# Eight sevens in each down product's first block, seven low parts by transfer, and retention's rotations moved behind its own products

## The chip, the cores and the metric

The kernel runs on one core of a Trainium2 chip, in one launch. Times are device microseconds of that core; a profiled execution also has a span, from its first to its last instruction. Lower is better.

## What is computed

One decoder layer over 256 tokens of width 2048, all in float32:

```python
h = layer_norm(alpha*h + 0.5*swiglu(h, w_ffn1_gu, w_ffn1_down))      # d_ff 5632
rq, rk, rv, rg, aq, ak, av, gate_r, gate_a = split(h @ w_in)
rq, rk = rotary(rq), rotary(rk) * dk**-0.5                           # 8 heads of 128
ret = (silu(rg) * head_group_norm(retention(rq, rk, rv))) @ w_ret_out
att = windowed_attention(rotary(aq), rotary(ak), av, sinks) @ w_att_out
mixed = (sigmoid(gate_r)*ret + sigmoid(gate_a)*att) @ w_mix_out
h = layer_norm(alpha*h + mixed)
h = layer_norm(alpha*h + 0.5*swiglu(h, w_ffn2_gu, w_ffn2_down))
h = layer_norm(alpha*h + sigmoid(h @ w_ple_gate) * (p @ w_ple_proj))
# swiglu(x) = (silu(x @ w_g) * (x @ w_u)) @ w_down
```

## The kernel before

**Split products.** Each float32 operand is cut into a high part (rounded to the matmul's format) and a low part, the rest. A product is three matmuls summed in PSUM: high x low, high x high, low x high (`Sum.add`, lines 426 to 428; the names begin with `h` and `l`). Weights arrive as raw chunks of 128 x 1024 (512 KB, `Chunk`, line 115, on SP's queue). `split` (lines 101 and 102) has ScalarE cast the high part and VectorE subtract to get the low one.

**Units.** A product over pairs of k (256 rows of weights) is a list of units, and `block` runs them in order. Each pair covers two weight chunks (two column halves n), two k and two token halves:

- `P`, plain: two `Single`, 24 matmuls of 512 columns.
- `F`, folded: the second chunk is a `Folded`. Its low part comes not from VectorE but from a transfer: ScalarE casts the high part (line 165), writes its negative as the low part (line 166), and GpSimd issues a DMA that adds the raw chunk onto it inside SBUF (line 167).
- `S`, seven: the pair's 2 x 2 x 2 block products are made as seven products (21 matmuls) on sums of the weights (`Seven.make`: four additions on VectorE, lines 222 to 225, then 3.5 chunks' worth of high and low parts) and on combinations of the activations (`seven_forms`). Four of the seven go to PSUM banks of their own; after a block's last seven the `fold` (`seven_common`, lines 533 to 537, then line 1056) adds these onto the outputs. That last seven runs its steps in another order, so that those four end first.

**The order around a block.** `plan` lists all weight units of the whole kernel. `done(u)` after a unit frees its slots and calls `fill`, which loads and prepares units ahead: it prepares while less than 45 matmuls are ready, and loads while less than 90 are under way, both only if the slots of `slots_for_weights` allow it. SBUF has 46 slots of 4 KB per partition for weights, activations and everything temporary. Engines work in program order, so a preparation that waits for a slot holds up what stands behind it on ScalarE and VectorE.

**The down products** (`ffn`, tiles `f1d` and `f1e`, `f2d` and `f2e`). The 5632 rows are 22 pairs in 11 groups of activations. The output is made in two blocks of two column halves each. `down_units` gives the order of the pairs: the first block has twelve plain pairs, then five sevens and five plain pairs in turn, a plain one last; the second has two plain pairs, eight sevens and plain ones in turn, and the rest. Four groups (`SEVEN_DOWN`, pairs 12 to 19) have combinations, made by `before_unit` in front of units 2, 4, 6 and 8 of the first block. `before_unit` also cuts one group of activations into high and low parts (`convert`) in front of every second unit. After the first block VectorE adds the plain sums onto the residual (line 1078) and takes statistics (line 798).

**Beside the products** `run_side` runs, once per unit, the next job of `side` and a step of the first generator in `lazy`. In the first down product that is the table of retention's rotary angles (`rotary_table("r")`); in the mixers the sums of weights for the second feed-forward product, made ahead and put into DRAM (`sums_ahead`, 10 pairs, 8 of them here), and the table for attention. Retention's queries and keys (tile `rqk`) are rotated at the end of each of eight groups (`rotate`: joined from PSUM, shuffled, two products, one sum). Further on four pairs of gate sums (`sig`, line 1460) are copied out of PSUM on ScalarE.

## Time and profile before

| | |
|---|---|
| median of 3 runs | 2252.4 us (2251.03 to 2253.74) |
| the profiled execution: time, span | 2251.64 us, 2249.9 us |
| granted TensorE clock | 0.999 |
| busy: TensorE, VectorE, ScalarE, GpSimd | 99%, 88%, 63%, 2% |
| DMA: mean rate | 248 GB/s |
| low parts by transfer | 43, in the gate-and-up products |

In the lines below a number in front is a time or a window in microseconds from the span's start; `PE` is TensorE, `PEld` its weight load, `DVE` VectorE, `ACT` ScalarE, `POOL` GpSimd. `out<-in` names tiles with their buffer numbers left out, x is a count, and a bracket or an arrow at the end tells how long the engine had waited and for whom. In the list of waits the numbers are the total, the times, and the longest.

### The profile page before, as it was taken

How to read it: one execution, taken by the hardware profiler on the slowest of the kernel's cores; microseconds unless marked ns; L12 is line 12 of the kernel's file. 1: busy time of each engine (PE TensorE's matmuls, PEld its weight loads, DVE VectorE, ACT ScalarE, POOL GpSimd, SP SyncE). 2: the span in 40 equal slices, each digit the busy share in tenths (PEclk: the TensorE clock that was granted, in tenths of full speed). 3: DMA queues.
4: the chain of work that ended last, by engine and by line, in shares of the span. 5: the costliest groups of instructions: out<-in, count | busy, mean ns of one | idle time of the engine just before them, and what ended most of it. 6: DMA issues, size and time to landing. Idle time of an engine off the chain costs nothing.

```text
span 2249.9 us, 28922 instructions
## 1 busy us (share of the span) xinstructions
PE 2230.0 (99%) x10191; PEld 1845.7 (82%) x10191; DVE 1976.5 (88%) x2575; ACT 1406.5 (63%) x1640; POOL 39.7 (2%) x52
## 2 busy tenths in 40 slices
PE   9999999999999999999999999999999999999998
PEld 8888878888888888888778888888888778888887
DVE  6999999999989887888789778789999899889877
ACT  6777777766555444656776466456667677655533
POOL 0000000000000000000000000000000000000000
PEclk9999999999999999999999999999999999999999
DMA  9989998965677878767666578788989898555771
GB/s 321 244 270 254 246 257 239 256 220 186 220 284 260 292 282 306 223 239 231 187 189 234 178 229 296 301 283 274 315 271 294 275 250 262 188 215 210 286 266 72
DMA packets 292267, 557.14 MB, mean 248 GB/s; under 512 B 92045, under 2 KB 96525, under 8 KB 292121
## 3 DMA queue, kind: packets, MB, share of 16 engines
q1 hardware_dynamic: 283944, 530.16, 70.5%
q0 software_dynamic: 6192, 22.55, 5.3%
q10 hardware_dynamic: 1984, 2.58, 0.4%
q8 instruction: 80, 1.31, 0.2%
q14 instruction: 67, 0.54, 0.1%
HBM read 484.43 MB, written 29.36 MB: 228 GB/s over the span
## 4 chain that ended last, share of the span: by engine, by line
PE 75%; DVE 10%; DMA 6%; ACT 4%; issue 4%; SPq 0%; ACTq 0%; DVEq 0%; POOLq 0%
DMA lf_gu<-rf_gu 3%; PE rqk L377 3%; PE f1g L428 2%; PE f1g L427 2%; PE f1g L426 2%; PE f2g L427 2%; PE f2g L426 2%; PE f2g L428 2%; PE f1u L428 2%; PE f1u L427 2%; PE f2u L428 2%; PE f1u L426 2%; DVE lw_in_f L102 2%; PE f2u L427 2%; PE f2u L426 2%
## 5 line engine op out<-in xcount | busy, mean ns | idle before, releaser
L102 DVE TENSOR_TENSOR lf_gu<-rf_gu,hf_gu 128x1024 fp32r<-128x1024 f32 (+1 forms) x225 | 267.7, 1210 | 20.5 <-ACT hf_gu L101 19.7
L101 ACT CAST hf_gu<-rf_gu 128x1024 fp32r<-128x1024 f32 (+1 forms) x225 | 228.5, 1039 | 33.3 <-DMA rf_gu<-in_f_gu 32.9
L102 DVE TENSOR_TENSOR lf_down<-rf_down,hf_down 128x1024 fp32r<-128x1024 f32 x150 | 178.8, 1220 | 19.1 <-ACT hf_down L101 18.2
L102 DVE TENSOR_TENSOR lw_in_f<-rw_in_f,hw_in_f 128x1024 fp32r<-128x1024 f32 x140 | 167.4, 1219 | 28.2 <-ACT hw_in_f L101 27.7
L101 ACT CAST hf_down<-rf_down 128x1024 fp32r<-128x1024 f32 x150 | 151.9, 1049 | 49.3 <-DMA rf_down<-in_f_down 19.5
L101 ACT CAST huf_gu<-uf_gu 128x1024 fp32r<-128x1024 f32 x76 | 80.1, 1054 | 120.6 <-DVE uf_gu L223 111.9
L101 ACT CAST hw_in_f<-rw_in_f 128x1024 fp32r<-128x1024 f32 x140 | 140.2, 1049 | 5.2 <-PE rg L428 1.5
L101 ACT CAST hvf_gu<-vf_gu 128x1024 fp32r<-128x1024 f32 x76 | 80.1, 1054 | 32.1 <-DVE vf_gu L225 31.3
L102 DVE TENSOR_TENSOR luf_gu<-uf_gu,huf_gu 128x1024 fp32r<-128x1024 f32 x76 | 92.6, 1218 | 0.0
L102 DVE TENSOR_TENSOR lvf_gu<-vf_gu,hvf_gu 128x1024 fp32r<-128x1024 f32 x76 | 92.5, 1218 | 0.0
L426 PE MATMUL f1g<-hf_gu,xt 128*128 128x512 f32 x232 | 90.7, 391 | 0.0
L428 PE MATMUL f1g<-lf_gu,xt 128*128 128x512 f32 x232 | 90.5, 390 | 0.1
L427 PE MATMUL f1g<-hf_gu,xt 128*128 128x512 f32 x232 | 90.5, 390 | 0.0
L426 PE MATMUL f2g<-hf_gu,ht 128*128 128x512 f32 x214 | 83.5, 390 | 0.0
L428 PE MATMUL f2g<-lf_gu,ht 128*128 128x512 f32 x214 | 83.3, 389 | 0.0
L427 PE MATMUL f2g<-hf_gu,ht 128*128 128x512 f32 x214 | 83.3, 389 | 0.0
L428 PE MATMUL f1u<-lf_gu,xt 128*128 128x512 f32 x192 | 75.4, 393 | 4.1 <-DMA lf_gu<-rf_gu 4.1
L427 PE MATMUL f1u<-hf_gu,xt 128*128 128x512 f32 x192 | 74.7, 389 | 0.0
L426 PE MATMUL f1u<-hf_gu,xt 128*128 128x512 f32 x192 | 74.7, 389 | 0.0
L167 POOL DMA_DIRECT2D lf_gu<-rf_gu x43 | 37.3, 868 | 1852.8 <-DMA rf_gu<-in_f_gu 1240.9
L428 PE MATMUL f2u<-lf_gu,ht 128*128 128x512 f32 x168 | 66.0, 393 | 2.7 <-DMA lf_gu<-rf_gu 2.5
L426 PE MATMUL f2u<-hf_gu,ht 128*128 128x512 f32 x168 | 65.8, 392 | 0.0
(1471 smaller groups left out, 6788.9 us busy)
## 6 DMA issues: line engine op xcount, KB each, us to landing
rf_gu<-in_f_gu SPq DMA_DIRECT2D x360, 512.0 KB
rf_down<-in_f_down SPq DMA_DIRECT2D x176, 512.0 KB
rw_in_f<-in_w_in_f SPq DMA_DIRECT2D x148, 512.0 KB
lf_gu<-rf_gu POOLq DMA_DIRECT2D x43, 512.0 KB, 7.5
rw_rv<-in_w_rv SPq DMA_DIRECT2D x32, 512.0 KB
rw_ret<-in_w_ret SPq DMA_DIRECT2D x32, 512.0 KB
rw_mix<-in_w_mix SPq DMA_DIRECT2D x32, 512.0 KB
rw_pg<-in_w_pg SPq DMA_DIRECT2D x32, 512.0 KB
```

What stands on the lines that cost most here:

```text
L101: act.copy(dst_hi, src)
L102: (lo_engine or dve).tensor_tensor(dst_lo, src, dst_hi, ALU.subtract)
L167: pool.dma_start(c.lo, c.raw, accum_op=ALU.add)
L377: pe.matmul(ps[f], hi[:, kk, f * P : (f + 1) * P], rhs(k), start=k == 0, stop=k == n_k - 1,)
L426: pe.matmul(o, al, bh, start=first, stop=False)
L427: pe.matmul(o, ah, bh, start=False, stop=False)
L428: pe.matmul(o, ah, bl, start=False, stop=self.left == 0)
```

## The change

Both first blocks of the down products get the order `FIRST_DOWN`: six plain pairs, two folded, then eight sevens with a folded or plain pair between them; two of the sevens stand next to each other, and the block ends in a seven. Five of its pairs are folded. The second block keeps its eight sevens, moved back by one pair, and gets two folded pairs (`SECOND_DOWN`); its fold and tail stay. Groups of activations are converted four units (`LEAD`) before their first use, and the low part is issued behind the four combinations where both fall on one unit. `Folded.make` writes the negative from the raw chunk, issues the transfer, and casts the high part last; this holds for every folded unit of the kernel. The rotary table of retention is made in the mixers; the groups are only joined at their ends, and a second list of generators, `slow`, makes the table, then the rotations in place, then attention's table, one step per unit beside a step of `lazy`. The sums ahead are cut into three and five pairs. The last two of the four pairs of gate copies go to VectorE.

```diff
@@ -48,6 +48,10 @@
 
 SEVEN_DOWN = (6, 7, 8, 9)
 
+FIRST_DOWN = "PPPPPPFFSFSPSFSPSFSSPS"
+SECOND_DOWN = "PPPSPSPSFSPSFSPSPSPPPP"
+LEAD = 4
+
 BIG = 3.0e38
 MAGIC = 12582912.0
 INV_2PI = 0.15915494309189535
@@ -162,9 +166,9 @@
         def make(self):
             c = self.chunk
             c.make_hi()
+            act.mul(c.lo, c.raw, -1.0)
+            pool.dma_start(c.lo, c.raw, accum_op=ALU.add)
             act.copy(c.hi, c.raw)
-            act.mul(c.lo, c.hi.bitcast(F32), -1.0)
-            pool.dma_start(c.lo, c.raw, accum_op=ALU.add)
 
     class Turn:
 
@@ -356,15 +360,16 @@
         room["quiet"] = on
 
     side = []
-    lazy = []
+    lazy, slow = [], []
     idle = lambda: None
 
     def run_side(n=1):
         for _ in range(n):
             if side:
                 side.pop(0)()
-        if lazy and next(lazy[0], "end") == "end":
-            lazy.pop(0)
+        for jobs in (slow, lazy):
+            if jobs and next(jobs[0], "end") == "end":
+                jobs.pop(0)
 
     def features_chunk(key, n_k, rhs, ps):
         c, chunks = key[-1], n_k // 4
@@ -489,7 +494,7 @@
             if p == sevens[-1]:
                 fold(p1.ap, p6.ap, p7.ap, q5.ap)
 
-    def seven_forms(full, hi, lo):
+    def seven_forms(full, hi, lo, between=None):
 
 
         a11, a21 = (full[:, 0::2, t * P : (t + 1) * P] for t in range(2))
@@ -500,6 +505,8 @@
         dve.tensor_tensor(f7, a11, a21, ALU.subtract)
         dve.tensor_tensor(f6, f5, a11, ALU.subtract)
         dve.tensor_tensor(f3, a12, f6, ALU.add)
+        if between is not None:
+            between()
         split(hi, lo, raw)
         return lambda e: [(hi[:, 2 * j + e, :], lo[:, 2 * j + e, :]) for j in range(4)]
 
@@ -918,24 +925,16 @@
     def down_units(n_held):
 
 
-        first = [("P", p) for p in range(2 * SEVEN_DOWN[0])]
-        g = SEVEN_DOWN[0]
-        sevens = [2 * h for h in SEVEN_DOWN[:3]] + [2 * SEVEN_DOWN[2] + 1, 2 * SEVEN_DOWN[3]]
-        plain = [p for p in range(2 * g, KF // 2) if p not in sevens]
-        plain = [p for p in plain if p < 2 * SEVEN_DOWN[2]] + sorted(
-            (p for p in plain if p >= 2 * SEVEN_DOWN[2]), key=lambda p: p < 2 * SEVEN_DOWN[3] + 2
-        )
-        while sevens or plain:
-            for kind, of in (("S", sevens), ("P", plain)):
-                if of:
-                    first.append((kind, of.pop(0)))
-        plain = [p for p in range(KF // 2) if p // 2 not in SEVEN_DOWN]
-        second = [("P", p) for p in plain[:2]]
-        rest = plain[2:]
-        for g in SEVEN_DOWN:
-            for e in range(2):
-                second += [("S", 2 * g + e), ("P", rest.pop(0))]
-        return first, second + [("P", p) for p in rest[:-n_held]], rest[-n_held:]
+        sevens = [2 * g + e for g in SEVEN_DOWN for e in range(2)]
+        plain = [p for p in range(KF // 2) if p not in sevens]
+        first, second = [], []
+        for out, order in ((first, FIRST_DOWN), (second, SECOND_DOWN)):
+            n = order.count("S")
+            of = {"S": sevens[:n], "P": sorted(plain + sevens[n:], key=lambda p: (p in sevens, p))}
+            of["F"] = of["P"]
+            out += [(kind, of[kind].pop(0)) for kind in order]
+            assert not of["S"] and not of["P"]
+        return first, second[:-n_held], [p for _, p in second[-n_held:]]
 
     def down_keys(name, b):
         return lambda n, p: (name + "_down", 2 * b + n, p)
@@ -973,10 +972,14 @@
 
         acts = {}
 
+        def convert_high(g):
+            hi, lo = (slot([P, 4, S], F32R, f"{name}a{w}{g}") for w in "hl")
+            act.copy(hi, raws[g])
+            acts[g] = hi, lo
+            return lambda: dve.tensor_tensor(lo, raws[g], hi, ALU.subtract)
+
         def convert(g):
-            hi, lo = (slot([P, 4, S], F32R, f"{name}a{w}{g}") for w in "hl")
-            split(hi, lo, raws[g])
-            acts[g] = hi, lo
+            convert_high(g)()
 
         for j in range(KF // 4):
             pg, pu = banks(f"{name}g{j}"), banks(f"{name}u{j}")
@@ -1056,17 +1059,27 @@
                     dve.scalar_tensor_tensor(x, x, 2.0 * ALPHA, v, ALU.mult, ALU.add)
             return f
 
+        when = {}
+        for at, (kind, p) in enumerate(first):
+            if p // 2 > 1:
+                when.setdefault(p // 2, max(0, at - LEAD))
+
         def before_unit(u):
-            if u == 0 and name == "f1":
-                lazy.append(rotary_table("r"))
-            g = u // 2 + 2
-            others(2 * KF // 4 - max(0, KF // 4 - 1 - g) + (2 if u >= 10 else 0))
-            if u % 2 == 0:
-                if 2 <= u < 2 + 2 * len(SEVEN_DOWN):
-                    at = u // 2 - 1
-                    made[SEVEN_DOWN[at]] = seven_forms(raws[SEVEN_DOWN[at]], space[:, 2 * at], space[:, 2 * at + 1])
-                if g < KF // 4:
-                    convert(g)
+            new = [g for g in when if when[g] == u]
+            others(2 * KF // 4 - (KF // 4 - len(acts) - len(new)) + (2 if u >= 10 else 0))
+            lows = [convert_high(g) for g in new]
+
+            def convert_low():
+                for f in lows:
+                    f()
+
+            if u % 2 == 0 and 2 <= u < 2 + 2 * len(SEVEN_DOWN):
+                at = u // 2 - 1
+                made[SEVEN_DOWN[at]] = seven_forms(
+                    raws[SEVEN_DOWN[at]], space[:, 2 * at], space[:, 2 * at + 1], convert_low
+                )
+            else:
+                convert_low()
             if u in (11, 12):
                 y[u - 11] = load_columns(residual, u - 11, name + "y")
 
@@ -1121,14 +1134,16 @@
             dve.tensor_tensor(v[:, f], ps[f][:, :S], lo[:, f], ALU.add)
         return v
 
-    def rotate(ps, name, dst, cos, sin, shuffle):
-        q = joined(ps, name)
+    def turn_by_angle(q, name, dst, cos, sin, shuffle):
         qs = half(name + "sh")
         dve.stream_shuffle(qs, q, shuffle)
         c, s = (v[:, None, :].broadcast_to([P, 2, S]) for v in (cos, sin))
         dve.tensor_tensor(q, q, c, ALU.mult)
         dve.tensor_tensor(qs, qs, s, ALU.mult)
         dve.tensor_tensor(dst, q, qs, ALU.add)
+
+    def rotate(ps, name, dst, cos, sin, shuffle):
+        turn_by_angle(joined(ps, name), name, dst, cos, sin, shuffle)
 
     SH_R = [(i + 16) % 32 for i in range(32)]
     SH_A = [i + 8 if i < 8 else i - 8 if i < 16 else i for i in range(32)]
@@ -1170,7 +1185,6 @@
         side.insert(n, job)
 
     def mixers(ht, norm, residual, keepers, away):
-        cos_r, sin_r = trig["r"]
         rhs = lambda k: (ht[:, k, :S], ht[:, k, S:])
         both_halves = lambda k: ht[:, k, :]
         rq = [slot([P, 4, S], F32, f"rq{j}") for j in range(2)]
@@ -1178,7 +1192,20 @@
 
         def rotated(grp, ps):
             who = (rq, rk)[grp // 4][grp % 4 // 2]
-            rotate(ps, f"rr{grp}", who[:, grp % 2 * 2 : grp % 2 * 2 + 2, :], cos_r, sin_r, SH_R)
+            to = who[:, grp % 2 * 2 : grp % 2 * 2 + 2, :]
+            joined(ps, f"rr{grp}", to)
+            unturned[grp] = to
+
+        unturned = {}
+
+        def rotations():
+            for grp in (0, 4, 1, 5, 2, 6, 3, 7):
+                while grp not in unturned:
+                    yield
+                to = unturned.pop(grp)
+                turn_by_angle(to, f"rr{grp}", to, *trig["r"], SH_R)
+                yield
+                yield
 
         rv = []
 
@@ -1201,10 +1228,14 @@
         values(0, ps)
         slots_for_weights(14)
         ahead = [(gu_keys("f2", j)(0, p), gu_keys("f2", j)(1, p)) for j in AHEAD for p in AHEAD[j]]
-        lazy.append(sums_ahead(ahead[:2], 3, 2))
-        lazy.append(rotary_table("a"))
-        lazy.append(sums_ahead(ahead[2:5], 2, 2))
-        lazy.append(sums_ahead(ahead[5:8], 2, 3))
+        def angles():
+            yield from rotary_table("r")
+            yield from rotations()
+            yield from rotary_table("a")
+
+        slow.append(angles())
+        lazy.append(sums_ahead(ahead[:3], 3, 2))
+        lazy.append(sums_ahead(ahead[3:8], 2, 2))
         for grp in range(8):
             ps = banks(f"rqk{grp}")
             features_out([(("w_in_f", grp), ps)], KD, both_halves)
@@ -1457,7 +1488,7 @@
             paired_out(("w_in_f2", 21 + 2 * j), KD, rhs, ps, before)
             sig.append(slot([P, 2, 512], F32, f"sig{j}"))
             for t in range(2):
-                act.copy(sig[-1][:, t], ps[t])
+                (act.copy if j < 2 else dve.tensor_copy)(sig[-1][:, t], ps[t])
         assert not side
 
         def mixer_block(name, units, keys, lhs):
```

## The prediction

> **What bounds the kernel now.** First the page: span, then busy time.
>
> ```profile
> span 2249.9 us, 28922 instructions
> PE 2230.0 (99%) x10191; PEld 1845.7 (82%) x10191; DVE 1976.5 (88%) x2575; ACT 1406.5 (63%) x1640; POOL 39.7 (2%) x52
> ```
>
> TensorE is busy 2230.0 of 2249.9 us. Time can therefore go in two ways only: fewer matmuls, or fewer of its few waits. The waits of TensorE, longest first:
>
> ```profile
> PE f1u L428 <- DMA lf_gu<-rf_gu: 4.1, 6, 1.8
> PE ao L1423 <- ACT apt L197: 3.2, 2, 2.5
> PE f2u L428 <- DMA lf_gu<-rf_gu: 2.5, 3, 1.8
> ```
>
> Two of the three largest are waits for the low part that comes by transfer (`lf_gu<-rf_gu`, the folded unit): 4.1 us in 6 and 2.5 us in 3, none over 1.8 us. The third, the attention's 3.2 us, the change leaves alone.
>
> Then the stages around the edits (columns: window, length, then busy us and count of PE, PEld, DVE, ACT, POOL, the granted clock, DMA share, GB/s). 240 to 463.6 is part of the first gate-and-up product; 463.6 to 694 and 1915.8 to 2147 are the two down products, first and second block; 720 to 814 retention's query and key products, 1156 to 1237 the gate blocks.
>
> ```profile
> 240.00:463.60 223.60, 220.42 (x969) 181.19 (x968) 207.49 (x245) 166.20 (x177) 12.97 (x15) 1.00 0.89 252
> 463.60:579.90 116.30, 116.30 (x515) 96.30 (x514) 107.97 (x135) 72.22 (x76) 0.00 (x0) 1.00 0.60 203
> 579.90:694.00 114.10, 114.10 (x505) 94.49 (x504) 105.53 (x125) 61.53 (x66) 0.00 (x0) 1.00 0.71 253
> 720.00:814.00 94.00, 94.00 (x533) 82.37 (x533) 83.77 (x121) 45.71 (x60) 0.00 (x0) 1.00 0.82 295
> 1156.00:1237.00 81.00, 81.00 (x359) 67.05 (x358) 79.78 (x95) 52.46 (x59) 0.00 (x0) 1.00 0.65 215
> 1915.80:2032.00 116.20, 116.20 (x514) 96.24 (x513) 102.36 (x116) 71.17 (x74) 0.00 (x0) 1.00 0.57 200
> 2032.00:2147.00 115.00, 115.00 (x513) 95.23 (x512) 106.80 (x128) 61.49 (x68) 0.00 (x0) 1.00 0.69 248
> ```
>
> TensorE is at 100% in all but the first, at clock 1.00. VectorE follows closely: 107.97 of 116.30, 105.53 of 114.10, 83.77 of 94.00, 79.78 of 81.00. So matmuls are what is to be saved, and VectorE is what can spoil it.
>
> **Part 1: three more sevens in each first block.** A plain pair is 24 matmuls of 512 columns (two weight chunks, two k, two token halves, three products for the split), a seven is 21.
>
> ```profile
> L426 PE MATMUL f1d<-hf_down,f1al x141: 389/389/389, 463.8 to 579.4; 128*128 128x512 f32 x141
> L426 PE MATMUL f1e<-hf_down,f1al x120: 389/389/389, 580.1 to 693.7; 128*128 128x512 f32 x120
> ```
>
> A matmul's 389 ns is its pipelined length. Its spacing is what counts: the first block, 17 x 24 + 5 x 21 = 513 matmuls by the code, begins at 463.8 and the next at 580.1, so 116.3 / 513 = 0.227 us each. The first block goes from five sevens to eight in both products; the second keeps eight and only changes order. 2 x 3 x 3 x 0.227 = **4.1 us less**.
>
> What VectorE pays (timeline of VectorE, start and length):
>
> ```profile
> 560.69 0.69 DVE L222 TENSOR_TENSOR uf_down<-rf_down,rf_down 128x512 f32<-128x512 f32 x1
> ...
> 567.36 2.35 DVE L102 TENSOR_TENSOR lf_down<-rf_down,hf_down 128x1024 fp32r<-128x1024 f32 x2
> ...
> 1957.33 0.42 DVE L499 TENSOR_TENSOR sums<-f2a 128x256 f32<-128x256 f32 x1
> ```
>
> A seven's preparation runs from 560.69 to 567.36, 6.7 us, the pair behind it 2.35 us (about 2.3 without the overlap): 9.0 us of VectorE for 45 matmuls, 10.2 us of TensorE. A transferred low part takes 1.1 us off a pair. For one product: 3 x (6.7 - 2.3) - 7 x 1.1 = +5.5 us. In the first product the rotary table leaves: 107.97 against 102.36 for the same work in the second says 5.6 us. VectorE then has about 213 of 228 us in the first product and 215 of 229 in the second: it fits on average. The dense place is the last 14 units of the first block: eight sevens (53.4), three plain (6.8), three folded (3.4), five low parts of activations (5.7) and one set of combinations (four of 0.42 and a subtraction, 2.8) make 72.1 us against (8 x 21 + 6 x 24) x 0.227 = 70.7 us. It falls behind by 1.4 us there, from whatever lead it has. How much that is:
>
> ```profile
> 569.90 0.39 PE L426 MATMUL f1d0s<-hf_down,f1al 128*128 128x512 f32 x1
> 569.91 2.00 ACT L101 CAST hf_down<-rf_down 128x1024 fp32r<-128x1024 f32 x2 [1.48 <-PE f1d L427]
> ```
>
> The seven prepared by about 567.4 starts at 569.90: 2.5 us of lead, and its last sums are read only after 17 matmuls, 3.9 us later. ScalarE at 569.91 had waited for TensorE, that is for slots: the preparation had run as far ahead as it could. 2.5 + 3.9 covers 1.4. I charge nothing for it; without that lead it costs what the third rival says.
>
> **Part 2: the block now ends in a seven.** Until now a plain pair stood behind the last seven and hid its fold; now the fold meets the next block's start.
>
> ```profile
> 573.27 0.59 ACT L533 COPY eve<-f1d0s 128x512 f32<-128x512 f32 x1 [1.35 <-PE f1d L427]
> 573.89 0.69 DVE L534 TENSOR_TENSOR evw<-eve,f1d0s 128x512 f32<-128x512 f32 x1 [0.53 <-ACT eve L533]
> 578.81 2.35 DVE L102 TENSOR_TENSOR lf_down<-rf_down,hf_down 128x1024 fp32r<-128x1024 f32 x2
> 581.08 2.48 DVE L1078 TENSOR_TENSOR f1y<-f1y,f1d 128x512 f32<-128x512 f32 x4
> 583.47 2.46 DVE L798 BATCH_NORM_STATS2 f1st<-f1y 128x6 f32<-128x512 f32 x4
> 585.85 0.67 DVE L222 TENSOR_TENSOR uf_down<-rf_down,rf_down 128x512 f32<-128x512 f32 x1
> 574.43 0.39 PE L428 MATMUL f1d<-lvf_down,f1ah 128*128 128x512 f32 x1
> 580.10 0.39 PE L426 MATMUL f1e<-hf_down,f1al 128*128 128x512 f32 x1
> ```
>
> The seven's last matmul issues at 574.43, so the unit ends at 574.66; the fold's copy had started 1.4 us before that, its six VectorE operations take 573.89 to 578.81, 4.9 us. The next block starts at 580.10, before the additions of the plain sums (581.08): its banks are those that the fold has freed, not those. With nothing between, its first matmuls need the bank of the copy (free at 573.86, in time) and 0.7 us later one more; the fold's second sum ends 573.89 + 1.4 = 575.3, 0.6 us after the unit: even. If instead that bank waits for all four sums (until 576.5), each product loses 1.2 us. I take 0.3 each, 0 to 1.2 the range. Behind it queue 2.5 us of additions, 2.5 us of statistics and two plain low parts: 4.2 + 4.9 + 2.3 + 6.7 = 18.1 us after the block's end for the next seven, which starts after three plain pairs, 16.3 us, and is read to its end 3.9 us later. 2.1 us are left.
>
> **Part 3: the folded unit's order.** The sign change now comes before the high copy, and the transfer starts one ScalarE operation earlier, in all 43 old folded units.
>
> ```profile
> 309.73 1.04 ACT L165 CAST hf_gu<-rf_gu 128x1024 fp32r<-128x1024 f32 x1
> 310.80 1.06 ACT L166 ACTIVATE lf_gu<-hf_gu 128x1024 fp32r<-128x1024 f32 x1
> 312.22 0.86 POOL L167 DMA_DIRECT2D lf_gu<-rf_gu  x1 [17.55 <-ACT lf_gu L166]
> 321.79 0.50 PE L428 MATMUL f1u<-lf_gu,xt 128*128 128x512 f32 x1 [1.81 <-DMA lf_gu<-rf_gu]
> 322.12 0.39 PE L426 MATMUL f1u<-hf_gu,xt 128*128 128x512 f32 x1
> DMA to landing us min/median/max: 4.9/7.5/10.3
> L167 POOL DMA_DIRECT2D lf_gu<-rf_gu x43: 859/862/1010, 41.6 to 1890.6; - x43
> ```
>
> Copy at 309.73, sign change at 310.80, issue at 312.22, read at 321.79 after 1.81 us of wait. Each transfer starts 1.07 us sooner (310.80 - 309.73). Of nine waits that add up to 6.6 us, none over 1.8, two keep about 0.75 us each and the others end: 5.1 us. A wait also hides 0.16 us that the profile counts as busy (389 - 227 ns) and is followed by one matmul 0.1 us late (322.12 - 321.79 - 0.23); seven such ends give 1.8 us more. Together 6.9 us if every landing moves with its start; 0 if none does. I take **6 us less**. The high part comes 1.06 us later than now, but still some 9 us ahead of the low one: nothing waits for it.
>
> The Trainium skill (DMA: Bandwidth & Descriptors, "Anatomy of one DMA — SWDGE (gpsimd) path") fits such a transfer at 2.0 us plus bytes over 436 GB/s, as an estimate 3.2 us for 512 KB. The trace disagrees: 4.9 to 10.3 us. By that page no folded unit would wait at all, and the new ones in the down products would cost nothing.
>
> Those are 14 new transfers. From the start of the sign change to the landing is 1.06 + 0.36 + 4.9 to 10.3 us; the next ScalarE cast waits for none of it. Second chunks are cast about 9 to 11 us before use (569.91 for 580.10), so most arrive in time, in a stage whose DMA share is 0.57 to 0.71. Bounds: 0, and 14 x 1.8 = 25 us if each waited as long as the worst old one; near the old rate after the shift (2 of 43) and some more for the shorter lead I take 0.8 us. POOL issues nothing else there; its issue took 859 to 1010 ns under a busy VectorE, so there is no queue to be behind.
>
> **Part 4: the rotations and the gate copies.** The first product's table leaves work that had no wait, so no time there.
>
> ```profile
> 737.65 0.74 DVE L1127 STREAM_SHUFFLE rr0sh<-rr0v 128x512 f32<-128x512 f32 x1
> 740.37 2.35 DVE L102 TENSOR_TENSOR lw_in_f<-rw_in_f,hw_in_f 128x1024 fp32r<-128x1024 f32 x2
> 1185.49 1.22 DVE L102 TENSOR_TENSOR lvw_in_f<-vw_in_f,hvw_in_f 128x1024 fp32r<-128x1024 f32 x1
> 1187.89 0.39 PE L428 MATMUL ga0s<-lvw_in_f,gaf1h 128*128 128x512 f32 x1
> ```
>
> A rotation is 740.37 - 737.65 = 2.7 us of VectorE. Into the stage of 720 to 814 come the retention table (5.6 us) and about one and a half more of the sums made ahead (four operations of 0.69 and two of 1.22 each, 7.8 us), which no longer pause for the attention's table; that table (5.6) and two rotations (5.4) fall behind the stage. 83.8 + 2.4 = 86.2 of 94 us, though its last groups carry two rotations each. TensorE had no wait there (94.00 of 94.00); 0 to 2 us now, I take 0.3. DMAs move with it: a small load of positions on ScalarE's queue, and on SP's the loads and stores of those sums, between weight loads, in a stage with a DMA share of 0.82. Two of the four pairs of gate copies go to VectorE; the last pair (2 x 0.69 us, the length of the fold's L534 on as many elements) lands ahead of the fullest stage, 79.78 of 81.00, whose last seven is ready at 1186.7 and read at 1187.89: 1.2 us of room for 1.4 us. Between no cost (ScalarE is freed of as much, and VectorE's next operation waits for its cast) and 1.4 us, I take 0.3, nearer to the row with the room.
>
> **The sum.** -4.1 - 6 + 0.6 + 0.8 + 0.3 + 0.3 = -8.1 us. The profiled execution took 2251.64 us, 1.74 more than its span and 0.76 less than the median of the runs, 2252.4; so 2243.5 on its own scale, **2244.3 us** as a median.
>
> **Rivals.** *The landing stays.* If transfers are held by what else the 16 engines carry (share 0.89 in the gate-and-up product) and not by their start, part 3 gives about 0.5 us and the rest stands: 2252.4 - 4.1 - 0.5 + 2.0 = 2249.8 us. For it: landings spread by 5.4 us. Against it: waits of at most 1.8 us behind transfers that differ this much look like the tail of one spread, and a shift of all cuts a tail. The Trainium skill says of the same page ("Issuing engines are not separate DMA queues") that transfers of every queue interleave on the same 16 engines; the spread agrees with that.
>
> *Added waits eat the gain.* The 14 transfers late by 0.3 us each, both boundaries at 1.2 and the mixers at 2: 4.2 + 2.4 + 2.3 against 10.1 leaves 2251.2 us.
>
> *VectorE is late in the dense stretch.* Low parts that come by transfer hold their raw slot until they land, up to 10.3 us; if the sevens' preparation waits for those slots, the lead of 2.5 us is gone when the stretch begins. Then its 1.4 us and the 9.8 us of fold, additions and statistics stand before the next seven uncovered, less 3.9 us: 7.3 us per product, 14.6 in all, 2244.3 + 14.6 = 2258.9 us. It decides once VectorE idles more than the lead, about 2.5 + 3.9 us, within the stretch. For it: ScalarE's wait for slots at 569.91. Against it: with 9.0 of 10.2 us per couple, VectorE caught up after each seven.
>
> **How the numbers follow.** Forecast 0.68, landing stays 0.12, waits eat the gain 0.10, VectorE late 0.10. The forecast's own cases run from 2241 (6.9 us, no new waits: -11 us) to 2248; the range goes up to 2251.5 to take in the next two. A measurement of this kernel tells about 0.2%, 4.5 us, from no change: faster than 2247.9 is the forecast and a little of the next, 0.70; slower than 2256.9 is the last, 0.09; the same 0.21.
>
> **What would show it.** In the changed profile: 9 matmuls fewer in each first block, which should last about 114.3 us; TensorE's wait for `lf_gu` near 1.5 us instead of 6.6, and no `lf_down` in that list above 1 us; at the end of each first block a gap under 1.2 us; no wait of TensorE in retention's products. Wrong would be: waits for `luf_down` or `lvf_down` (third rival), waits for `lf_gu` as before with the transfers 1.07 us longer (first), or a gap of several us before the second block.

## The result and the profile after

The changed kernel takes 2247.37 us in the median (2246.52 to 2252.30), the kernel before, run beside it, 2254.99 us (2251.03 to 2258.21): 7.6 us less between the two medians. The ratio of the runs is 0.9971 with a 95% interval of 0.9962 to 0.9980, which is 6.5 us less (4.5 to 8.6); the experiments below are compared by this ratio. The forecast was 8.1 us less (2252.4 to 2244.3).

The changed kernel's page and its waits of TensorE (in total, times, longest, us):

```profile
span 2248.5 us, 29078 instructions
PE 2230.2 (99%) x10173; PEld 1846.2 (82%) x10173; DVE 1987.0 (88%) x2601; ACT 1421.7 (63%) x1662; POOL 51.7 (2%) x66
PE f27s L433 <- DVE lf_gu L106: 2.1, 1, 2.1
PE lnps L684 <- DVE f2y L672: 1.0, 2, 0.6
PE lnps L684 <- DVE f1y L672: 0.9, 2, 0.5
PE gt L433 <- DVE lw_in_f L106: 0.8, 1, 0.8
PE f1u L433 <- DMA lf_gu<-rf_gu: 0.8, 1, 0.8
PE f27s L433 <- DVE luf_gu L106: 0.8, 1, 0.8
PE f2u L433 <- DMA lf_gu<-rf_gu: 0.4, 1, 0.4
```

TensorE executes fewer matmuls and waits little for `lf_gu`: 0.8 and 0.4 us, where 4.1 and 2.5 stood. But there are new names: `f27s` (pair 7's sevens in the second gate-and-up product) waits 2.9 us for VectorE, the layer norms' `lnps` 1.9 us for `f1y` and `f2y`, and `gt` 0.8 us for VectorE. The stages that were shown of before:

```profile
240.00:459.30 219.30, 219.30 (x969) 181.61 (x968) 206.47 (x245) 164.18 (x177) 12.93 (x15) 1.00 0.91 257
459.30:573.60 114.30, 114.30 (x506) 94.65 (x505) 105.53 (x123) 80.63 (x85) 4.33 (x5) 1.00 0.71 222
573.60:688.70 115.10, 114.67 (x505) 94.30 (x503) 105.36 (x126) 62.62 (x68) 1.72 (x2) 1.00 0.75 264
1913.90:2028.20 114.30, 114.30 (x506) 94.66 (x505) 105.31 (x123) 80.61 (x85) 4.33 (x5) 1.00 0.71 223
2028.20:2141.60 113.40, 112.66 (x496) 92.67 (x494) 105.12 (x125) 62.32 (x67) 1.91 (x3) 1.00 0.74 256
```

Both first down blocks last 114.3 us instead of 116.3 and 116.2; TensorE is full in them. The second blocks now have a gap at the end (114.67 of 115.10, 112.66 of 113.40), which the kernel before had not (114.10 of 114.10, 115.00 of 115.00).

The profiled execution took 2250.32 us, 3 us over its median, and that of before 2251.64 us, 3.4 us under its own. So the two spans differ by 1.4 us only, and the stages tell more. Lengths in us, from a stage's first matmul to the next one's (e1 has the folded unit's new order alone, e12 is the fastest version found; both come below):

| stage | before | after | e1 | e12 |
|---|---|---|---|---|
| first gate-and-up product | 458.48 | 454.00 | 454.21 | 454.18 |
| its down product, first block | 116.28 | 114.24 | 116.30 | 114.24 |
| second block and norm | 145.23 | 146.95 | 145.23 | 145.95 |
| retention | 326.12 | 325.36 | 326.10 | 325.35 |
| gates and gate blocks | 185.63 | 187.94 | 187.06 | 186.57 |
| rest of the mixers | 222.45 | 222.36 | 222.48 | 223.06 |
| second gate-and-up product | 456.45 | 457.79 | 456.70 | 456.63 |
| its down product, first block | 116.28 | 114.24 | 116.28 | 114.24 |
| second block, up to the gate's product | 115.16 | 117.39 | 115.17 | 115.17 |
| to the end | 102.44 | 102.93 | 102.45 | 102.42 |

In the changed kernel's column 1.6 us in the gates and 3.2 us in the second gate-and-up product are a halved clock that only some executions have at these places (last section); the gates of e1 and e12 hold 1.6 us of it too. Without it the changed kernel has: 4.5 less in the first product, 4.1 less in the first blocks, 0.8 less in retention, 1.9 less in the second product, 3.95 more in the second blocks with their norms, 0.7 more in the gates, 0.4 more after them. About 6 us less.

### The profile page after: what moved, and what is told of

It is laid out like the page before. It is cut to its first block, busy times and chain, and to the rows that moved or that the text cites. A ratio compares the mean times of both kernels' runs of the same rounds, so it can differ in the third digit from the quotient of the medians.

```text
span 2248.5 us, 29078 instructions
## 1 busy us (share of the span) xinstructions
PE 2230.2 (99%) x10173; PEld 1846.2 (82%) x10173; DVE 1987.0 (88%) x2601; ACT 1421.7 (63%) x1662; POOL 51.7 (2%) x66
## 4 chain that ended last, share of the span: by engine, by line
PE 90%; DVE 4%; DMA 3%; issue 2%; ACT 1%; ACTq 0%; POOL 0%; DVEq 0%; POOLq 0%
PE rqk L382 3%; PE f1g L431 3%; PE f1g L432 3%; PE f1g L433 3%; PE f2g L431 2%; PE f2g L432 2%; PE f2g L433 2%; PE f1u L433 2%; PE f1u L431 2%; PE f1u L432 2%; PE f2u L433 2%; PE f2u L431 2%; PE f2u L432 2%; PE aqk L382 2%; PE f1d L433 1%
## 5 line engine op out<-in xcount | busy, mean ns | idle before, releaser
L106 DVE TENSOR_TENSOR lf_down<-rf_down,hf_down 128x1024 fp32r<-128x1024 f32 x130 | 155.5, 1220 | 14.5 <-ACT hf_down L105 13.9
L105 ACT CAST hf_down<-rf_down 128x1024 fp32r<-128x1024 f32 x130 | 132.8, 1049 | 38.3 <-DMA rf_down<-in_f_down 26.9
L105 ACT CAST huf_down<-uf_down 128x1024 fp32r<-128x1024 f32 x32 | 33.7, 1053 | 57.2 <-DVE uf_down L227 55.2
```

What stands on the lines that cost most here:

```text
L105: act.copy(dst_hi, src)
L106: (lo_engine or dve).tensor_tensor(dst_lo, src, dst_hi, ALU.subtract)
```

## Experiments

The theory after this comparison: the folded unit's order carries the gain, and the down orders give back at the norms what they save. The rivals were that the landings would stay, that the parts work only together, and that VectorE's whole load, not the place of single steps, makes the new waits. Ratios below are to the kernel before, with 95% intervals.

**e1: the folded unit's order alone.**

```
-            act.copy(c.hi, c.raw)
-            act.mul(c.lo, c.hi.bitcast(F32), -1.0)
+            act.mul(c.lo, c.raw, -1.0)
             pool.dma_start(c.lo, c.raw, accum_op=ALU.add)
+            act.copy(c.hi, c.raw)
```

> Only the folded unit's new order (sign change, transfer, then high copy), on the kernel before. Theory (waits shrink with the earlier start): TensorE's waits for lf_gu fall from 6.6 us in nine to 1 to 2 us, and the time falls by 4 to 6 us, less what VectorE's own lateness in the second gate-and-up product takes back (0 to 2 us, seen as a longer wait of f27s for lf_gu from VectorE). Rival, the landing stays: the transfers last 1.07 us longer, the waits for lf_gu stay above 5 us, and the time falls by 0.5 us.

Measured: 2246.84 us, ratio 0.9969 (0.9959 to 0.9980): 7.0 us less, as much as the whole change brings and a little more than the 4 to 6 us expected. Its waits for `lf_gu` fall to 3.5 us, not to the 1 to 2 us expected:

```profile
PE f2u L428 <- DMA lf_gu<-rf_gu: 2.7, 3, 1.2
PE f1u L428 <- DMA lf_gu<-rf_gu: 0.8, 2, 0.4
```

The time from issue to landing of the `lf_gu` transfers hardly grew (e1's row follows: count, size, median us; before and in the changed kernel it is 7.5). The median is 0.3 us longer, not the 1.07 us of the earlier start, so the landings moved with their start, and the rival falls.

```profile
lf_gu<-rf_gu POOLq DMA_DIRECT2D x43, 512.0 KB, 7.7
```

The gain is not spread as the waits were. Over the profiled executions of this study with 46 shared slots the first gate-and-up product lasts 459.3 us with the old order (four, 458.2 to 460.7, one of them with 1.6 us of halved clock) and 454.0 with the new one (eight, 453.8 to 454.2); the second lasts 456.5 with either. There the folded waits stay in e1 (2.7 us), and in the changed kernel 2.9 us at `f27s` stand in their place. e9 asks why. So the traces place 5 of the 7 us; where the other 2 come from stays open.

**e2: the down orders alone** (`FIRST_DOWN`, `SECOND_DOWN`, `LEAD`, the low parts by transfer; old folded order; rotary table, rotations and gate copies as before).

> Only the down products' orders (eight sevens, seven plain pairs by transfer, the conversions' new lead), with the folded unit's old order, and the rotations and gate copies as before. Prediction's terms: each first block 2.04 us shorter, about 114.3 us, boundary 0.3 each, new transfers 0.8 in all: 2.7 us less altogether. Theory after the changed kernel's trace: both first blocks at about 114.3 us, but each second block with the layer norm behind it 1 to 1.7 us longer (waits of lnps for f1y and f2y), so only 1 to 2 us less altogether. Rival (the 14 transfers, starting 1.07 us later here than in the changed kernel, are late): waits of TensorE for lf_down in the first blocks of 0.3 us or more each, and no gain at all.

Measured: 2258.91 us, ratio 1.0018 (1.0009 to 1.0027): 4 us slower. The first block of the second MLP is 114.2 us, that of the first 119.5: there TensorE waits 3.3 us for one `lf_down`, with 1.6 us of halved clock behind it:

```profile
PE f1d L433 <- DMA lf_down<-rf_down: 3.3, 1, 3.3
```

Neither the prediction's term nor the theory had this; the rival's wait was there, in one place and not in all.

**e3: retention's rotations and tables and the gate copies alone.**

> Only retention's rotations and tables moved, and two pairs of gate copies on VectorE; the down products and the folded unit as before. Prediction's terms: 0.6 us more. Theory after the changed kernel's trace: nothing in retention's products, and a new wait of 0.8 to 1 us of the gate stage's first plain unit for VectorE's low part (gt for lw_in_f): 1 us more. Rival (VectorE is freed of 5.6 us in the first down product and that matters): 1 us less, with the first down product's blocks shorter than 116.3 and 114.1 us.

Measured: 2253.35 us, ratio 0.9998 (0.9989 to 1.0007), no difference that can be told; the 1 us more of the theory lies inside the interval. The new wait of `gt` is there with 0.8 us; against it, retention's stage is 0.8 us shorter, as in the changed kernel (there a wait of `ro` for `rsp`, 0.5 us in the kernel before, is gone). The first down product's blocks are not shorter: the rival falls.

So e1 + e2 + e3 give -7.0 + 4.1 - 0.5 = -3.4 us, not -6.5 (0.9971): the parts are not independent. Three more kernels complete the set.

**e7: everything but the folded unit's order.**

> The changed kernel with the folded unit's old order (high copy, sign change, transfer). The orders alone had cost 4 to 5 us, with one wait of 3.3 us for lf_down, the second folded unit of the first down product. Theory A (that unit was late because retention's rotary table stood in the same queues of VectorE and ScalarE; the table is gone here): its low part lands 1.07 us later than in the changed kernel, still some 5 us early, no wait for lf_down over 0.5 us, and the time is the changed kernel's plus what the reorder is worth alone, 2247.4 + 7.0 = 2254.4 us. Theory B (the old order's later start is what made it late): a wait for lf_down of about 3 us in the first down product again, and about 2258 us.

Measured: 2251.7 us, ratio 0.9999 (0.9991 to 1.0008), and no wait for `lf_down` at all in the first down product: theory A. Its number, 2254.4, was reckoned for a round in which the kernel before took 2254.99 us; here it took 2252.36. By the ratios the folded unit's order is worth 6.3 us beside the other parts (0.9999 against 0.9971), near the 7.0 that it brings alone.

**e13: everything but the fourth part.**

```
         def before_unit(u):
+            if u == 0 and name == "f1":
+                lazy.append(rotary_table("r"))
...
```

> The changed kernel without its fourth part: retention's rotary table stays in the first down product, its rotations and the gate copies are as in the kernel before; the down orders and the folded unit's new order are the change's. Theory A (the table makes the second folded unit late): its transfer starts 3 to 4 us later than in the changed kernel, counted from the first down product's start, and TensorE waits for lf_down there by 1 to 2.5 us; the wait of gt for lw_in_f is gone (1 us less); together 0 to 2 us more than the changed kernel, 2247.5 to 2249.5 us. Theory B (the old order made it late): no such wait, and 1 us less than the changed kernel, 2246.4 us.

Measured: 2255.67 us, ratio 1.0012 (1.0003 to 1.0021). Theory A again, and at a higher price than it said: 9 us more than the changed kernel (1.0012 - 0.9971). Of these the profiled execution has 6.6 us in the first block of the first down product (120.85 instead of 114.24 us), 1.6 of them a halved clock. The second folded unit of the first down product, in the changed kernel (ScalarE's sign change, the issue on POOL, and TensorE and DMA share while it is under way; the product begins at 459.33):

```profile
488.73 1.06 ACT L169 ACTIVATE lf_down<-rf_down 128x1024 fp32r<-128x1024 f32 x1
490.14 0.87 POOL L170 DMA_DIRECT2D lf_down<-rf_down  x1 [2.92 <-ACT lf_down L169]
490.10:495.20 5.10, 5.10 (x24) 4.21 (x24) 3.95 (x8) 3.14 (x4) 0.87 (x1) 1.00 0.78 150
```

and in e13 (the product begins at 459.27):

```profile
491.10 0.42 ACT L909 ACTIVATE trigr<-rotr 128x256 f32<-128x256 f32 x1 [1.26 <-DVE rotr L907]
493.31 1.05 ACT L169 ACTIVATE lf_down<-rf_down 128x1024 fp32r<-128x1024 f32 x1
494.72 0.87 POOL L170 DMA_DIRECT2D lf_down<-rf_down  x1 [4.59 <-ACT lf_down L169]
501.45 0.39 PE L432 MATMUL f1d<-hf_down,f1ah 128*128 128x512 f32 x1
504.44 0.50 PE L433 MATMUL f1d<-lf_down,f1ah 128*128 128x512 f32 x1 [2.61 <-DMA lf_down<-rf_down]
494.70:504.40 9.70, 6.29 (x27) 4.55 (x25) 8.41 (x14) 7.11 (x9) 0.87 (x1) 1.00 0.92 231
```

ScalarE reaches the sign change 34.0 us into the product instead of 29.4: ahead of it stand the rotary table's steps, on both engines (the one shown waits 1.26 us for VectorE). No other step of the fourth part runs in this product. While the table is unfinished the program also keeps two more slots from the weights (`others`, line 1043); no run separates this, but up to the sign change ScalarE waits for VectorE alone. The transfer now starts in a window with a DMA share of 0.92 instead of 0.78 and takes 9.7 us instead of 5.1 (landing 504.4). TensorE, at the unit by 501.7, waits 2.6 us.

**e14: everything but the down orders.**

> The folded unit's new order and the fourth part (rotations, tables, gate copies) without the new down orders: with this run all the kernels of the three parts, but for no part, have been run. Theory (the orders' 4.1 us in the first blocks are given back at the two norms, so they are worth 0 to 1 us beside the other two parts): the two parts add, 7.0 + 0.5, and the ratio to the kernel before is 0.9967, about 7.5 us less, the same as the changed kernel's within 1 us. Rival (the parts work only together; the orders bring their 4 us where the other two are there): 2.5 to 3.5 us less than the kernel before, a ratio of 0.9986.

Measured: 2247.21 us, ratio 0.9972 (0.9960 to 0.9983), close to the theory's 0.9967 and level with the changed kernel. With the folded order in place, the down orders bring 0 us with the fourth part (0.9971 against 0.9972) and cost 10 us without it (1.0012 against 0.9969). Between e2 and e13, where the table is left in its place, the folded unit's order brings only 1.4 us (1.0018 against 1.0012); why so little stays open.

**e6: the second block's sevens one place earlier.**

```
-SECOND_DOWN = "PPPSPSPSFSPSFSPSPSPPPP"
+SECOND_DOWN = "PPSPSPSFSPSFSPSPSPPPPP"
```

> The changed kernel with the second block's sevens one place earlier (plain, plain, seven, ... and five plain pairs at the end, as in the kernel before). Theory (the last seven's fold now ends one plain pair, 5.4 us, nearer to the norm, and its additions make f1y and f2y late): the waits of lnps for f1y and f2y, 1.0 and 0.9 us in the changed kernel, go, and 2 us less than the changed kernel, unless the first seven of the second block, whose preparation led by only 1.7 us at its place, is now late: that would be a wait of TensorE for uf_down or luf_down of up to 3.7 us per product, 5.4 us of plain pair minus 1.7 us of lead, and 2 x 3.7 - 2 = 5 us more than the changed kernel. Rival (the norm's wait comes of VectorE's whole load and not of the place of the last seven): the waits stay and the time is the same.

Measured: 2248.14 us, ratio 0.9971 (0.9961 to 0.9981), the changed kernel's. The norms' waits are gone, which speaks against the rival although it named the same time; in their place stand these:

```profile
PE f1d1s L433 <- DVE lf_down L106: 1.9, 1, 1.9
PE f2d1s L433 <- DVE lf_down L106: 1.8, 1, 1.8
```

The place of the last seven makes the norm late, and the place of the first seven makes that seven itself late. Why the last one counts (VectorE's fold and its addition to the plain sums, before the first norm): in the kernel before

```profile
677.27 0.68 DVE L534 TENSOR_TENSOR evw<-eve,f1d1s 128x512 f32<-128x512 f32 x1
689.10 0.69 DVE L1105 TENSOR_TENSOR f1y<-f1y,f1e 128x512 f32<-128x512 f32 x1 [0.36 <-PE f1e L428]
694.34 0.49 PE L677 MATMUL lnps<-ident,f1y 128*128 128x128 f32 x3
```

VectorE's second addition waits for TensorE: it has room, the fold began 17.1 us before `lnps`. In the changed kernel

```profile
676.15 0.68 DVE L541 TENSOR_TENSOR evw<-eve,f1d1s 128x512 f32<-128x512 f32 x1
685.26 0.67 DVE L1118 TENSOR_TENSOR f1y<-f1y,f1e 128x512 f32<-128x512 f32 x1
687.88 0.39 PE L433 MATMUL f1e<-lf_down,f1ah 128*128 128x512 f32 x1
688.78 0.42 PE L684 MATMUL lnps<-ident,f1y 128*128 128x128 f32 x2 [0.51 <-DVE f1y L672]
```

the fold begins 12.6 us before `lnps`, the addition waits for nothing, and `lnps` comes 0.9 us after the last product instead of 0.23: it waits for VectorE. The five us between 17.1 and 12.0 (12.6 less the wait) are about the plain pair. How much is lost varies: in the five other kernels with this order of the second block `f1y` is waited for at most 0.4 us and `f2y` 0.9 to 2.2.

**e10: the last two sevens next to each other**, the first where the change put it.

```
-SECOND_DOWN = "PPPSPSPSFSPSFSPSPSPPPP"
+SECOND_DOWN = "PPPSPSPSFSPSFSPSSPPPPP"
```

> The changed kernel with the second block's last two sevens next to each other and five plain pairs behind them (first seven where the change put it). Theory (the norm's waits come of the place of the last seven alone, and VectorE has slack before it, 1.6 to 2.3 us in gaps): no wait of lnps for f1y and f2y, no wait at the first seven, 2 us less than the changed kernel. Rival (two sevens in a row are 13.4 us of VectorE for 9.5 us of TensorE and the second is late): a new wait for uf_down or luf_down of up to 3 us per product, 4 us more than the changed kernel.

Measured: 2245.19 us, ratio 0.9962 (0.9948 to 0.9976). No wait of `lnps` for `f1y` or `f2y`, none for any seven of the down products: the theory. The two stages of the second blocks are 2.7 us shorter than in the changed kernel (145.79 and 115.82 us). The times alone would not show it: 0.0009, 2 us as expected, is inside the intervals.

**e4: all gate copies on ScalarE.**

```
-                (act.copy if j < 2 else dve.tensor_copy)(sig[-1][:, t], ps[t])
+                act.copy(sig[-1][:, t], ps[t])
```

> The changed kernel with all four pairs of gate copies back on ScalarE. Theory: the wait of gt for lw_in_f (0.8 us of wait, 1.1 us with the doubled spacing of a matmul behind it) comes of the two pairs on VectorE and goes; the stage of the gate products is 1.0 us shorter, and the time 1 us less. Rival (the wait comes of retention's tables and rotations that now stand behind the stage): the wait stays, and ScalarE's copies make the gate blocks wait for 0.5 us more.

Measured: 2246.47 us, ratio 0.9968 (0.9959 to 0.9978); the difference to the changed kernel is inside the intervals, but the wait of `gt` is gone and the stage from the first gate product to the gate blocks lasts 104.06 us, not 104.61, although its last 1.5 us run at half clock in e4, which costs about 0.7 us. The low part for which `gt` waited, in the changed kernel and (second fence) in e4:

```profile
1136.63 1.22 DVE L106 TENSOR_TENSOR lw_in_f<-rw_in_f,hw_in_f 128x1024 fp32r<-128x1024 f32 x1
1137.90 0.50 PE L433 MATMUL gt<-lw_in_f,ht 128*128 128x512 f32 x1 [0.79 <-DVE lw_in_f L106]
```

```profile
1133.95 1.22 DVE L106 TENSOR_TENSOR lw_in_f<-rw_in_f,hw_in_f 128x1024 fp32r<-128x1024 f32 x1
```

Counted from the first gate product (1045.88 and 1044.44) VectorE starts it at 90.75 and at 89.51 us: 1.24 us earlier without the copies, about the two of 0.69 that one pair costs. Part of this is lost further on in e4's execution: the norm behind the mixers waits 1.4 us for `mixy`, which it does not in the changed kernel's.

**e9: a slot of its own for the second MLP's transposed tiles.** The wait of `f27s` comes down a chain. The words of pair 6's transpose in the kernel before are copied and the transpose is issued at once:

```profile
1754.83 1.99 ACT L181 COPY wf<-evw 128x1024 uint16<-128x1024 uint16 x2
1756.85 1.93 SPq L185 DMA_TRANSPOSE mf<-wf  x1
```

In the changed kernel it is issued 2.3 us after its words:

```profile
1751.97 1.99 ACT L185 COPY wf<-evw 128x1024 uint16<-128x1024 uint16 x2
1756.26 1.91 SPq L189 DMA_TRANSPOSE mf<-wf  x1
1758.27 0.96 SPq L119 DMA_DIRECT2D rf_gu<-in_f_gu  x1
SPq L189 <- PE f2u L433: 7.6, 1, 7.6
1773.81 0.69 DVE L226 TENSOR_TENSOR uf_gu<-rf_gu,rf_gu 128x512 f32<-128x512 f32 x1 [8.05 <-DMA rf_gu<-in_f_gu]
1777.75 0.50 PE L433 MATMUL f27s<-lf_gu,ht 128*128 128x512 f32 x1 [2.07 <-DVE lf_gu L106]
```

By the waits in the program, the transposed tile `mf` now gets the slot of a folded unit's low part and waits for the last matmul that reads it; in the kernel before (whose folded units release their slots in another order) it got one that VectorE had long released. The traces agree: this transpose is issued 1.9 to 3.2 us after its words in all eight kernels with the new folded order and shared slots, and at once in the four with the old order. Behind the transpose on SP stands the load of pair 7's last seven (`rf_gu`, issued at 1758.27). It is this load for which VectorE idles 8 us, and for VectorE TensorE.

```
+    turned = ctx.enter_context(tc.tile_pool(name="turned", bufs=1))
...
-SLOTS = 46
+SLOTS = 45
...
-            self.moved = slot([P, 2, self.a, self.b, P], U16, "m" + self.name)
+            if self.name.startswith("f2"):
+                self.moved = turned.tile(shape, U16, tag="moved", name="m" + self.name)
+            else:
+                self.moved = slot(shape, U16, "m" + self.name)
```

> The changed kernel with a slot of its own for the second MLP's transposed tiles (45 shared slots instead of 46). Theory (in the changed kernel the sixth transpose gets the slot of a folded unit's low part and waits for the last matmul that reads it, 2.3 us longer than for its own data; behind it in SP's queue stands the load of the last seven of pair 7): the transpose is issued as soon as its words are copied, that load some 2 us earlier, the waits of f27s for VectorE (3.0 us in the changed kernel) fall below 1.5 us, the second gate-and-up product lasts 454.5 to 455.5 us instead of 457.8, and the time is 2 us less than the changed kernel. Rival (VectorE's whole load makes f27s late, and the folded waits that went are only moved there): f27s waits as before and the time is the same or, with a slot fewer for weights, up to 2 us more.

Measured: 2249.97 us, ratio 0.9984 (0.9974 to 0.9993): the chain was right, and yet the kernel is not faster for it; it looks 2.9 us slower than the changed kernel (0.0013, at the edge of what the intervals can tell).

```profile
1751.18 1.93 SPq L194 DMA_TRANSPOSE mf<-wf  x1
PE f2u L438 <- DMA lf_gu<-rf_gu: 3.2, 3, 1.8
PE f27s L438 <- DVE luf_gu L107: 0.2, 1, 0.2
```

Counted from the stage's first matmul the transpose is issued 3.0 us earlier, at once behind its words. The wait of `f27s` shrinks from 3 us to 0.4, and the stage lasts 455.4 us (453.6 in e11, 455.6 to 457.8 in the others with the new folded order). But the folded waits are 3.2 us here, and in the second down product the waits for `f2y` are 2.2 us, where the changed kernel has 1.0; here a halved clock, 1.6 us, follows them. That the missing shared slot costs this was not tried by itself, and its profiled execution is 1.8 us under its median: what the other executions lose stays open.

**e11: the edits of e4, e9 and e10 together.**

> The three edits together: own slot for transposes, gate copies on ScalarE, the last two sevens next to each other. Theory: the three terms add, 2 + 1 + 2: 5 us less than the changed kernel, 12 us less than the kernel before. Rival (each wait removed is followed by another a little later, as the folded waits were in the second gate-and-up product): 2 us less than the changed kernel at most.

Measured: 2243.97 us, ratio 0.9956 (0.9942 to 0.9971): 3.4 us less than the changed kernel, between the two.

**e12: the edits of e4 and e10.**

> The changed kernel with the last two sevens of the second block next to each other and all gate copies on ScalarE, slots as before. Theory (the two terms add: 2.2 and 0.9 us less, measured each alone): 2244.3 us. Rival (what is won in the gate stage is lost by the next late wait): 2245.2 us, as with the order alone.

Measured: 2241.76 us, ratio 0.9952 (0.9938 to 0.9966), 10.8 us less than the kernel before and faster than both it and the changed kernel; lower than the theory's 2244.3, but that number too belongs to a kernel before of 2254.99 us, of which it is 0.9953: by the ratio the two terms add. The difference to the changed kernel, 0.0019, is just clear of the noise (both intervals together allow 0.0017). Against e1 (0.9969) it is 3.8 us: here the gain of the down orders, 4.1 us in Part 1, comes through almost whole, as far as the intervals can tell. In the table above its second block and norm is still 0.7 us over e1's, the boundary of Part 2: TensorE waits there 0.5 us for the fold's sum `evw`.

## Why the prediction was right, and where it was wrong

**The scale.** The profile that the sum started from lay 0.76 us under the median of three runs; under the median of the runs beside the changed kernel it lies 3.4 us. The time of 2244.3 is 3.1 us low, 2.6 of them for that reason. The difference, 8.1 us, is not touched by it; it stands against 7.6 us by the medians and 6.5 by the ratio.

**Part 1** was right in the first blocks to 0.1 us (114.3), and VectorE kept up in the dense stretch. The step that failed is "the second keeps eight and only changes order", with no price. The order moves the last seven one plain pair nearer to the norm; its waits and what follows cost 3.95 us less the boundaries' 0.7, 3.2 us in all in the profiled execution. In e6, e10, e11 and e12, where the last seven stands one place earlier, no norm waits for `f1y` or `f2y`; in all six kernels with the change's order one waits for `f2y`.

**Part 2** took 0.3 us for each boundary. Spacing of the first matmuls of the second blocks (first product, then second):

```profile
574.02 0.39 PE L433 MATMUL f1e<-lf_down,f1ah 128*128 128x512 f32 x1
574.40 0.50 PE L431 MATMUL f1e<-hf_down,f1al 128*128 128x512 f32 x1
2029.25 0.50 PE L431 MATMUL f2e<-hf_down,f2al 128*128 128x512 f32 x1 [0.20 <-DVE evw L541]
```

574.40 comes 0.15 us late and its successor 0.11; in the second product it is 0.36 and 0.11. So 0.26 and 0.47: right. That "2.1 us are left" for the next seven was right in kind: one place earlier (e6) it is 1.9 us late.

**Part 3** took 6 us; the new order brings 7.0 alone and 6.3 beside the other parts, so the size was right. That two waits keep 0.75 us each was close (0.8 and 0.4). What was wrong is where: the traces show 5.3 us in the first gate-and-up product and in the mean none in the second, where the new order gives a transpose a slot that is released later. The sum considered engines and queues, not which slot a later tile would get. By the estimate of 3.2 us from the fit of the Trainium skill (DMA: Bandwidth & Descriptors, "Anatomy of one DMA — SWDGE (gpsimd) path") no folded unit would have waited and the order would have brought nothing; the runs disagree, with a median of 7.5 us in the changed kernel as before. The 14 new transfers were charged 0.8 us and cost none, with a median of 5.1 us.

**Part 4** failed at "leaves work that had no wait, so no time there". It holds in the kernel before (e3: no difference) and not with the new orders, whose folded units stand in the table's place: there it is worth 9 us (e13). The part was charged 0.6 us as an extra and is a condition of Part 1. The gate copies cost more than the 0.3 us taken: their stages are 0.7 us longer than before, and taking the copies alone back (e4) shortens them by 1.25, near the bound of 1.4. The wait came at `gt`, not at the gate blocks where the prediction looked. For the rotations the sign was wrong: retention gains 0.8 us where 0.3 of loss was taken.

**The rivals.** The landings did not stay (e1). VectorE was not late in the dense stretch. "Added waits eat the gain" is the nearest: 0.7 at the boundaries, 3.2 at the norms, 0.7 in the gates, 4.6 us in all, of which the norms were not in its list. It did not decide. The total came out near for a reason that is partly luck: the norms' 3.2 us, which the sum lacked, stood against 0.8 us of transfers that cost nothing, 1.1 us in retention that came as gain instead of loss, and 0.4 us more in the gate-and-up products of this execution. So the stages add up to 6 us, 2 less than the sum.

## What to carry to other kernels

Where an order is moved, follow its last element to what reads it next, not only its first to what prepares it: here one place in a list cost at the norms most of what three fewer matmuls per seven had saved. Where tiles share slots, a change in the order of release hands later tiles other slots; look which ones then wait for a late reader, and what stands behind them in an in-order queue. Parts that look like idle housekeeping can be the condition of another part, which only a run without them shows.

## What the runs showed of the hardware

After a wait of TensorE of about 2 us the granted clock sometimes drops to half for 3.4 us (6.8 once). In the changed kernel (matmuls, then a window):

```profile
1149.69 0.66 PE L1454 MATMUL ao<-apt,akv 128*64 128x256 f32 x4 [2.38 <-ACT apt L201]
1151.30 0.63 PE L433 MATMUL ga0a<-lw_in_f,ht 128*128 128x512 f32 x1
1151.72 0.63 PE L431 MATMUL ga0b<-hw_in_f,ht 128*128 128x512 f32 x1
1151.00:1154.00 3.00, 3.00 (x9) 2.32 (x8) 2.92 (x5) 1.91 (x3) 0.00 (x0) 0.50 0.73 245
```

Matmuls start 0.42 us apart instead of 0.23; in 3.4 us some eight start, so one such stretch costs 8 x 0.2 = 1.6 us. The kernel before has the same wait for `apt`, 2.5 us, at the same place, and goes on at full speed behind it:

```profile
1155.60:1159.00 3.40, 3.40 (x16) 2.77 (x16) 3.29 (x6) 3.22 (x7) 0.00 (x0) 1.00 0.75 248
```

In e6 it follows the 1.9 us wait for the first seven:

```profile
587.31 0.50 PE L433 MATMUL f1d1s<-lf_down,f1ah 128*128 128x512 f32 x1 [1.91 <-DVE lf_down L106]
588.00:591.00 3.00, 3.00 (x9) 2.33 (x8) 3.00 (x3) 2.61 (x4) 0.00 (x0) 0.50 0.00 0
```

In the fourteen profiled executions 39 gaps between two matmuls were over 1.5 us longer than the spacing (start-up and end left out), and right at 16 of them the clock halved, 9 times at the long wait for `apt` that each of the fourteen has. The shortest such gap was 1.9 us over the spacing. The Trainium skill (TensorE: Matmul & The Clock Gate, "What's actually happening") gives a free-running window of 3413 ns and a clock that is full or half, nothing between; the stretches of 3.4 and 6.8 us at 0.50 agree. Its rule of no gaps over about 3 us (section "Why this matters for your kernels") is not enough here: all but one of the 16 gaps were of 1.9 to 2.8 us.

The traces also show why the same wait halves the clock in one execution and not in another. In all fourteen every stretch between two changes of the clock is a whole number of 3.413 us (from 7.31 to 1150.77 us, 335 of them, in the changed kernel). Laid onto this grid, the 12 of the 39 gaps that had 2.07 us or more inside one window all halved the clock, the 18 with less than 1.86 us in any window never did, and of the 9 between these two 4 did. The wait for `apt` had 2.33 us in one window in the changed kernel; in the kernel before it fell on a boundary, 1.55 us on one side and 1.13 on the other.

For reading profiles it means that one profiled execution can be off by several us: up to its last 10 us such stretches cost the changed kernel's 4.8 us, and that of the kernel before nothing.
